# w_o of a one-core hybrid layer: half of its contraction by seven block products

## The chip, the cores and the metric

The kernel runs on one core of a Trainium2 chip. The metric is the device time of one execution in microseconds (us). Before the change the median of 3 runs is 1099.74 us (1099.03 to 1099.78).

## The reference

One layer with D = 1024 on 512 tokens, all in float32:

```
u = rms_norm(h, mix_pre_g);  q, k, v, xr, xg = split(u @ w_in)
y_a = (rg_lru(causal_conv(xr)) * gelu(xg)) @ w_lru_out
y_b = sliding_window_attention(q, k, v, sinks, bias) @ w_attn_out
g = sigmoid(u @ w_gate + b_gate)
merged = g[A] * y_a + g[B] * y_b
h = h + rms_norm(merged @ w_o, mix_post_g)
```

Ahead of this and behind it stands an FFN, h = h + 0.5 * rms_norm((silu(x @ w1) * (x @ w3)) @ w2), with x = rms_norm(h). The change is in `merged @ w_o`, a product of 512 x 1024 by 1024 x 1024.

## The kernel before

**Splitting.** Each float32 operand is held as a high part (rounded to the format that TensorE takes) and a low part (the rest). A product is three matmuls: high by high, high by low, low by high. ACT makes the high part by a copy, DVE the low part by a subtraction. Weights come tile by tile (128 x 1024): SP loads the raw tile (L150), ACT and DVE split it (L191, L192), in the order of a list that `get` walks through. `split2` (L226, L227) does the same for other operands.

**What sets the order.** The program is written out in Python, one instruction stream for each engine, and each engine runs its stream in order. `point()` is called at steps of the PE stream; `later(n, fn, rank)` has `fn` written out n points later. So the numbers in such calls decide where a piece of ACT, DVE or POOL work stands in its stream.

**Ahead of w_o.** Eight groups (tile f, L237 to L239, 24 matmuls of 128x512 each) multiply the attention's output by w_attn_out. Behind each group `mg_out` merges the branches: two DVE steps (L1780, L1781), then the high part on ACT (L1783) and the low part on DVE (L1784), which give tile mg. Each mg is one contraction tile of w_o. In this time the first pair of FFN2 weights (w1b, w3b) is prepared as well: POOL forms sums of raw w1b blocks (L890 to L896), and ACT and DVE split them (`pairs_b.prep`).

**w_o itself** (`tok_gemm`, L255 to L257, tile acc). The output is token major: 4 token tiles of 128 by 2 column halves of 512, so 8 banks of PSUM. All 8 contraction tiles are done classically: 8 x 4 x 2 x 3 = 192 matmuls of 128x512, the last two contraction tiles token by token. When a token tile is done, its norms follow (ACT sums of squares L310 and L334, DVE L311, L322 and so on), then transposes (tr, L355) into uT. The first four groups of FFN2 (tiles 0 and 1 of w1b and w3b) fill PE while the norms run.

**Block products.** For FFN1's w2 and FFN2's w2 a class `Halves` does part of the contraction by seven products in place of eight (Strassen and Winograd). It pairs contraction tiles p and q and views them as a 2 x 2 block matrix: b11, b12, b21, b22 of 2 x 128 rows by 512 columns, and the activations (hEO) as even and odd halves of 256 tokens. Weight blocks are combined as b12 - b11 and so on: `T` copies a block with factor -1 on ACT (L653), and a DMA that adds, issued by POOL, brings the other block from DRAM (L654). Activation sums are DVE steps `S` (L649). A unit (`unit`, L732 to L734, tile hw) is one product: 2 x 2 x 3 = 12 matmuls of 128x512 for one pair. `out` copies banks to SBUF (tile hc), and the norms add them later.

A tile of `BY_CAST` comes without a raw tile: POOL issues a DMA that rounds on the way (L147, high part), ACT writes the negative (L172), and a second POOL DMA adds the original to it (L174, low part).

Of the kernel before, what the change touches and what calls it, by code (L numbers as in the profile page):

```python
# [51 lines left out]
def hybrid_layer(ctx: ExitStack, tc: tile.TileContext, a: dict, out: bass.AP):  # L52
# [80 lines left out]
    want("wo", range(8))  # L133
# [162 lines left out]

    def post_norm(acc, t, gpost, scale, dst, after=None, last=False, eps=D * EPS, mid=None, part=None, ns=(0, 1)):
# [3 lines left out]
        junk = slot([P, D], name="junk")  # L301
# [24 lines left out]
    def norms(acc, t, gpost, scale, gpre, spill, eps, mid=None, part=None, ns=(0, 1)):  # L326

        hg = slot([P, D], name="hg")
        junk = slot([P, D], name="junk")
# [48 lines left out]
    def tok_gemm(nm, xs, n, R, gpost_name, scale, gpre_name, first, x_to=None, xf=None, spill=False, then=None, eps=None, pre=None):  # L378
# [35 lines left out]
        ep = lambda t: D * EPS if eps is None else eps[:, t : t + 1]  # L414
# [19 lines left out]
        if pre:  # L434
            G = pre.G
            pre.hooks[3 * G].append(vectors)
            pre.hooks[4 * G + 2].append(lambda: act.activation(small(1, "tiny"), veps[:, 0:1], AF.Abs_reciprocal_sqrt))
            pre.hooks[4 * G].append(lambda: act.activation(g[1], g[1], AF.Copy, scale=NEWT))
            x0 = st["get"] + len(tail)
            for i, u in enumerate(X_AT):  # L440
                pre.hooks[u].append(lambda i=i: dma_to(x0 + i + 1))
# [7 lines left out]
            for t in range(2):  # L449
                acc[t] = [pre.bank["bc"][t], pre.bank["bx"][t]]  # L450
                for n_ in range(2):
                    classical(t, n_)
            pre.prep(5 * G + LEAD + 2)
            x_split(0)
            norm(0, lambda: x_split(1))
            pre.cap = 7 * G - 2
            for u in range(5 * G, 6 * G):
                pre.step(u)
            pre.cap = 7 * G
            for t in range(2, 4):  # L460
                acc[t] = [pre.bank["bu"][t - 2], bank("acc")]
                classical(t, 1)
            pre.prep(7 * G)
            pre.hid.eo.clear()
            x_split(2)
            norm(1)
            for u in range(6 * G, 7 * G):
                pre.step(u, (0,))
            trs[0] = transpose_mm(us[0])
            transpose_out(trs[0], 0)  # L470
            classical(2, 0)
            for u in range(6 * G, 6 * G + 2):
                pre.step(u, (1,))
# [5 lines left out]
            for u in range(6 * G + 2, 7 * G):  # L479
                pre.step(u, (1,))  # L480
# [1392 lines left out]
GPOST_AT = 26  # L1873


RO = 6

NC1 = 4

# [56 lines left out]
```

## Time and profile before

| | |
|---|---|
| median of 3 runs | 1099.74 us |
| profiled execution | 1099.59 us |
| its span | 1097.7 us |
| granted TensorE clock | 0.998 |
| eight groups of w_attn_out | 670.98 to 714.53 us |
| w_o, classical products | 714.53 to 759.84 us, transposes among them |
| first matmul of FFN2's pairs | 784.14 us |

A row of the timeline gives start, length, engine, line, operation and tiles; a bracket behind it is the time that the engine stood idle before, and what ended that. Matmuls overlap, so the distance of two starts is their price, and not the length in the row. "Landing" is the time from the issue of a DMA to the arrival of its data.

### The profile page before, as it was taken

What the parts mean: (1) busy time and instruction counts of PE and PEld (TensorE: products, weight loads), DVE (VectorE), ACT (ScalarE), POOL (GpSimd) and SP (SyncE); (2) the same over time, 40 slices, a digit from 0 to 9 for tenths busy, and PEclk for the clock granted to TensorE, in tenths of its full rate; (3) what the DMA queues carried; (4) which work ended last, traced back from release to release, by engine and by line L of the source; (5) the groups of instructions that cost most, each with busy time, mean ns of one, the idle gap of its engine ahead of it and who ended that gap; (6) DMA issues with size and microseconds to landing.
All of it is one profiled execution on the core that took longest, in us unless ns stands there. A gap on an engine that the chain in (4) does not pass through costs nothing.

```text
span 1097.7 us, 18111 instructions
## 1 busy us (share of the span) xinstructions
PE 1089.5 (99%) x6856; PEld 986.9 (90%) x6856; DVE 927.0 (84%) x1334; ACT 704.0 (64%) x1226; POOL 398.3 (36%) x352
## 2 busy tenths in 40 slices
PE   9999999999999999999999999999999999999997
PEld 8899999998889878899888888888999999998885
DVE  5887999989997998887778866767889989889996
ACT  7756555588767778656656654446555455578872
POOL 0144933232102513242444443010977656633200
PEclk9999999999999999999999999999999999999999
DMA  9325663389866652157232335452323323449923
GB/s 339 122 81 140 126 158 100 115 184 232 238 167 210 162 151 74 39 178 242 65 91 79 117 133 211 138 187 88 126 78 116 106 88 110 144 103 241 211 77 134
DMA packets 53895, 156.46 MB, mean 143 GB/s; under 512 B 5536, under 2 KB 7456, under 8 KB 53808
## 3 DMA queue, kind: packets, MB, share of 16 engines
q1 hardware_dynamic: 40272, 122.49, 33.0%
q0 software_dynamic: 13248, 32.29, 15.7%
q8 instruction: 54, 0.88, 0.3%
q10 hardware_dynamic: 288, 0.52, 0.1%
q14 instruction: 33, 0.27, 0.1%
HBM read 139.57 MB, written 13.62 MB: 140 GB/s over the span
## 4 chain that ended last, share of the span: by engine, by line
PE 99%; DMA 0%; DVE 0%; ACT 0%; issue 0%; DVEq 0%; ACTq 0%
PE c L842 13%; PE c L843 13%; PE c L844 13%; PE f L237 10%; PE f L238 10%; PE f L239 9%; PE hw L732 6%; PE hw L733 6%; PE hw L734 6%; PE acc L257 1%; PE acc L255 1%; PE acc L256 1%; PE pt L1696 1%; PE s L1660 1%; PE s L1659 1%; PE tr L355 1%
## 5 line engine op out<-in xcount | busy, mean ns | idle before, releaser
L843 PE MATMUL c<-uT,wlo 128*128 128x256 f32 x516 | 146.0, 283 | 0.0
L844 PE MATMUL c<-uT,whi 128*128 128x256 f32 x516 | 146.0, 283 | 0.0
L842 PE MATMUL c<-uT,whi 128*128 128x256 f32 x516 | 146.0, 283 | 0.0
L842 PE MATMUL c<-Xh,whi 128*128 128x256 f32 x504 | 142.7, 283 | 0.0
L843 PE MATMUL c<-Xh,wlo 128*128 128x256 f32 x504 | 142.6, 283 | 0.0
L237 PE MATMUL f<-uT,whi 128*128 128x512 f32 (+1 forms) x380 | 138.5, 364 | 0.0
L238 PE MATMUL f<-uT,wlo 128*128 128x512 f32 (+1 forms) x380 | 136.9, 360 | 0.0
L239 PE MATMUL f<-uT,whi 128*128 128x512 f32 (+1 forms) x380 | 136.9, 360 | 0.0
L844 PE MATMUL c<-Xl,whi 128*128 128x256 f32 x456 | 129.1, 283 | 0.0
L227 DVE TENSOR_TENSOR wlo<-S,whi 128x1024 fp32r<-128x1024 f32 x86 | 120.9, 1406 | 4.7 <-ACT whi L226 2.5
L226 ACT ACTIVATE whi<-S 128x1024 fp32r<-128x1024 f32 x86 | 88.5, 1055 | 29.1 <-DVE S L891 28.0
L843 PEld LDWEIGHTS c<-uT,wlo 128*128 128x128 f32 x516 | 99.0, 192 | 0.2
L842 PEld LDWEIGHTS c<-uT,whi 128*128 128x128 f32 x516 | 99.0, 192 | 0.2
L844 PEld LDWEIGHTS c<-uT,whi 128*128 128x128 f32 x516 | 99.0, 192 | 0.0
L842 PEld LDWEIGHTS c<-Xh,whi 128*128 128x128 f32 x504 | 96.8, 192 | 0.3 <-issue 0.3
L843 PEld LDWEIGHTS c<-Xh,wlo 128*128 128x128 f32 x504 | 96.8, 192 | 0.0
L734 PE MATMUL hw<-whi,uT 128*128 128x512 f32 x228 | 88.7, 389 | 0.0
L732 PE MATMUL hw<-whi,uT 128*128 128x512 f32 x228 | 88.7, 389 | 0.0
L844 PEld LDWEIGHTS c<-Xl,whi 128*128 128x128 f32 x456 | 87.5, 192 | 0.0
L733 PE MATMUL hw<-wlo,uT 128*128 128x512 f32 x216 | 84.0, 389 | 0.0
L237 PEld LDWEIGHTS f<-uT,whi 128*128 128x128 f32 x380 | 71.8, 189 | 11.8 <-issue 1.4
L239 PEld LDWEIGHTS f<-uT,whi 128*128 128x128 f32 x380 | 71.7, 189 | 11.0
(435 smaller groups left out, 3181.8 us busy)
## 6 DMA issues: line engine op xcount, KB each, us to landing
raw_w1b<-in_w1b_dram SPq DMA_DIRECT2D x22, 512.0 KB, 4.2
raw_w3b<-in_w3b_dram SPq DMA_DIRECT2D x22, 512.0 KB, 4.4
raw_w3a<-in_w3a_dram SPq DMA_DIRECT2D x21, 512.0 KB, 4.4
raw_w1a<-in_w1a_dram SPq DMA_DIRECT2D x20, 512.0 KB, 4.5
raw_w2a<-in_w2a_dram SPq DMA_DIRECT2D x17, 512.0 KB, 5.5
raw_wg<-in_wg_dram SPq DMA_DIRECT2D x16, 512.0 KB, 4.1
raw_w2a<-in_w2a_dram POOLq DMA_DIRECT2D x15, 512.0 KB, 10.0
raw_w2b<-in_w2b_dram SPq DMA_DIRECT2D x15, 512.0 KB, 6.9
```

What stands on the lines that cost most here:

```text
L226: act.activation(hi, src, AF.Copy)
L227: dve.tensor_tensor(out=lo, in0=src, in1=f32(hi), op=ALU.subtract)
L237: pe.matmul(ps[:, c0:c1], wh[:, s], h_, start=k == 0 and c0 == 0, stop=False, skip_group_check=True)
L238: pe.matmul(ps[:, c0:c1], wl[:, s], h_, start=False, stop=False, skip_group_check=True)
L239: pe.matmul(ps[:, c0:c1], wh[:, s], l_, start=False, stop=k == KT - 1, skip_group_check=True)
L255: pe.matmul(acc[n], x[:, 0, c], wh[:, s], start=first, stop=False, skip_group_check=skip)
L732: pe.matmul(ps, xs[:, 0, j, c], hi[:, j, :], start=start and j == 0, stop=False, skip_group_check=True)
L733: pe.matmul(ps, xs[:, 0, j, c], lo[:, j, :], start=False, stop=False, skip_group_check=True)
L734: pe.matmul(ps, xs[:, 1, j, c], hi[:, j, :], start=False, stop=i == self.G - 1, skip_group_check=True)
L842: pe.matmul(ps, wh[:, s], xh, start=first, stop=False, skip_group_check=True)
L843: pe.matmul(ps, wl[:, s], xh, start=False, stop=False, skip_group_check=True)
L844: pe.matmul(ps, wh[:, s], xl, start=False, stop=k == 3, skip_group_check=True)
```

## The change

The contraction tiles 0 to 3 of w_o go through `Halves` with one pair of pairs (`GS_W`), tiles 4 to 7 stay classical (`TAIL_W`). In order on PE: units u0 to u4 (m1, m5, m2, m6, m3), classical products of token tiles 0 and 1 into the same banks, u5 (m7), classical token tiles 2 and 3 (second half), u6 (m4), with transposes and the remaining classical products between its parts. With `fold`, m2 and m3 behave differently from before: their banks receive the earlier partial sums by a DVE addition in place (L819 in the new numbering), ahead of the classical products, and so the norms of token tiles 0 and 1 don't add them. The norms of tile 1 are written out right behind those of tile 0, with u5 (m7) inside them; those of tile 2 have the second transposes' copies inside.

`mg_out` halves only mg of tiles 4 to 7 into high and low; tiles 0 to 3 go whole into hEO. The factor 0.5 is dropped and made good by 4 times the epsilon in the norms. The weight operands of w_o's units are formed in three ways: `weight` splits a block in SBUF (u1, u3), `fetch` and `rest` take a plain block from DRAM by a rounding and an adding DMA (u0, u2, u4), `T` and `w7` form the combined blocks. The tiles 0 and 1 of w1b and w3b come by `BY_CAST`. The w1b pair's five steps of preparation stand at other points (`PB_AT`, `PBW_AT`), and the loads of h and the splits of wo4 to wo7 in hooks of the units (`MARKS_W`).

```diff
-    want("wo", range(8))
+    want("wo", TAIL_W)
...
+            if pre.fold:
+                for t in range(2):
+                    acc[t] = [pre.bank["bc"][t], pre.bank["bx"][t]]
+                    for n_ in range(2):
+                        classical(t, n_)
+                pre.prep(7 * G)
+                x_split(0)
+                norm(0, lambda: x_split(1))
+                x_split(2)
+                norm(1, lambda: [pre.step(u) for u in range(5 * G, 6 * G)])
+                for t in range(2, 4):
+                    acc[t] = [pre.bank["bu"][t - 2], bank("acc")]
+                    classical(t, 1)
+                pre.hid.eo.clear()
+                for u in range(6 * G, 7 * G):
+                    pre.step(u, (0,))
+                trs[0] = transpose_mm(us[0])
+                transpose_out(trs[0], 0)
+                x_split(3)
+                classical(2, 0)
+                for u in range(6 * G, 7 * G):
+                    pre.step(u, (1,))
+                trs[1] = transpose_mm(us[1])
+                norm(2, lambda: transpose_out(trs[1], 1))
+                for t in range(2):
+                    transpose_xf(trs[t], t, xf)
+                classical(3, 0)
...
+        def w7(self, i):
+            if self.once("w7", i):
+                dve.tensor_tensor(out=self.raw["b11", i], in0=self.raw["b22", i], in1=self.raw["b11", i], op=ALU.subtract)
+
+        def fetch(self, u):
+            b, i = self.OPERANDS[self.names[u // self.G]][0], u % self.G
+            hi, lo = slot([P, 2, 512], F32R, name="whi"), slot([P, 2, 512], F32R, name="wlo")
+            pool.dma_start(out=hi, in_=self.src(b, i))
+            self.parts[u] = hi, lo
+
+        def rest(self, u):
+            b, i = self.OPERANDS[self.names[u // self.G]][0], u % self.G
+            hi, lo = self.parts[u]
+            act.activation(lo, f32(hi), AF.Copy, scale=-1.0)
+            pool.dma_start(out=lo, in_=self.src(b, i), accum_op=ALU.add)
+
+        def weight(self, u):
+            b, i = self.OPERANDS[self.names[u // self.G]][0], u % self.G
+            hi, lo = slot([P, 2, 512], F32R, name="whi"), slot([P, 2, 512], F32R, name="wlo")
+            split2(hi, lo, self.raw[b, i])
+            self.parts[u] = hi, lo
...
-                if m == "m7":
-                    dve.tensor_tensor(out=o, in0=ps, in1=o, op=ALU.add)
+                if m not in ("m1", "m5", "m6"):
+                    dve.tensor_tensor(out=o if m == "m7" else ps, in0=ps, in1=o, op=ALU.add)
...
-        act.activation(m[:, 0, :], t, AF.Copy, scale=0.5)
-        dve.scalar_tensor_tensor(out=m[:, 1, :], in0=t, scalar=0.5, in1=f32(m[:, 0, :]), op0=ALU.mult, op1=ALU.subtract)
-        mg.append(m)
+        if i in TAIL_W:
+            m = mixed.t[i] = slot([P, 2, SEQ], F32R, name="mg")
+            act.activation(m[:, 0, :], t, AF.Copy)
+            later(1, lambda: dve.tensor_tensor(out=m[:, 1, :], in0=t, in1=f32(m[:, 0, :]), op=ALU.subtract), 0)
...
+    half_w.load(1)
+    half_w.loads.pop()
+    half_w.fetch(0)
+    for n, fn in zip(W_AT, (
+        lambda: half_w.t1(0), lambda: half_w.rest(0), lambda: half_w.fetch(2), lambda: half_w.t2(0), lambda: half_w.rest(2),
+        lambda: half_w.weight(1), lambda: half_w.w7(0), lambda: half_w.t4(0), lambda: half_w.prep(1, False), lambda: half_w.prep(2, False),
+        lambda: half_w.weight(3), lambda: half_w.prep(3, False), lambda: half_w.fetch(4), lambda: half_w.prep(4, False), lambda: half_w.rest(4),
+    )):
+        later(n, fn, 2)
...
-RO = 6
+TAIL_W = (4, 5, 6, 7)
+GS_W = ((0, 2),)
+PB_AT = (1, 3, 5)
+PBW_AT = ((3, 2), (4, 3))
+W_AT = (2, 2, 4, 5, 6, 7, 8, 9, 9, 10, 11, 11, 12, 13, 14)
+MARKS_W = (1, 2, 3, 3), (3, 4, 5, 5)
+XW_AT = (1, 2, 3, 4)
```

The first place is POOL's stream while the groups of w_attn_out run. OL is the low part of the attention's output, S are the sums of w1b blocks. Before:

```order
L1732 TENSOR_TENSOR OL_7020<-o_7269,OH_7019 128x2x128
L895 TENSOR_TENSOR S_1458_7369<-raw_w1b_1451_7342 128x512
L896 TENSOR_TENSOR S_1458_7369<-S_1458_7369,raw_w1b_1450_7340 128x512
L890 TENSOR_TENSOR S_1459_7370<-raw_w1b_1450_7340,S_1458_7369 128x512
L891 TENSOR_TENSOR S_1459_7370<-raw_w1b_1450_7340,raw_w1b_1451_7342 128x512
L294 DMA bc_mix_post_g_7749<-in_mix_post_g_dram 128x1024
```

After (raw_wo are the blocks b12, b22 and t4 of w_o in turn, whi and wlo the parts of u0's, u2's and u4's weights):

```order
L968 TENSOR_TENSOR S_1475_7363<-raw_w1b_1450_7340,raw_w1b_1451_7342 128x512
L691 DMA raw_wo_7380<-in_wo_dram 128x2x512
L724 DMA wlo_7347<-in_wo_dram 128x2x512
L717 DMA whi_7424<-in_wo_dram 128x2x512
L691 DMA raw_wo_7452<-in_wo_dram 128x2x512
L724 DMA wlo_7425<-in_wo_dram 128x2x512
L691 DMA raw_wo_7526<-in_wo_dram 128x2x512
L717 DMA whi_7591<-in_wo_dram 128x2x512
L724 DMA wlo_7592<-in_wo_dram 128x2x512
L294 DMA bc_mix_post_g_7700<-in_mix_post_g_dram 128x1024
```

Eight DMAs on w_o now stand behind the sums of w1b, where POOL had nothing; one more (u0's high part, L717) stands ahead of them.

The second place is DVE's stream ahead of the classical products of w_o. Before:

```order
L1780 SCALAR_TENSOR_TENSOR g_7203<-g_7203,f_7612 128x512
L1781 TENSOR_TENSOR g_7203<-g_7203,g_4751 128x512
L1784 SCALAR_TENSOR_TENSOR mg_7684<-g_7203,mg_7684 128x512
L192 TENSOR_TENSOR wlo_7730<-raw_wo_1506_7610,whi_7729 128x1024
L192 TENSOR_TENSOR wlo_7734<-raw_wo_1522_7662,whi_7733 128x1024
```

After (hx is an activation operand of a unit, hw a bank, hc a bank's copy; raw_wo with one number is a block, with two a classical tile; hw_7742 is the bank of token tile 0, first half, hw_7706 its second half):

```order
L227 TENSOR_TENSOR wlo_7724<-raw_wo_7344,whi_7723 128x1024
L227 TENSOR_TENSOR hx_7725<-hEO_7409,hx_7725 128x512
L227 TENSOR_TENSOR wlo_7731<-S_1475_7363,whi_7730 128x1024
L192 TENSOR_TENSOR wlo_7735<-raw_wo_1538_7670,whi_7734 128x1024
L819 TENSOR_TENSOR hw_7742<-hw_7742,hc_7690 128x512
L227 TENSOR_TENSOR wlo_7759<-raw_wo_7526,whi_7758 128x1024
L227 TENSOR_TENSOR hx_7760<-hEO_7410,hx_7760 128x512
L227 TENSOR_TENSOR w_1570_7765<-raw_w1b_1451_7342,w_1570_7765 128x512
L192 TENSOR_TENSOR wlo_7769<-raw_wo_1539_7672,whi_7768 128x1024
L192 TENSOR_TENSOR wlo_7773<-raw_wo_1540_7674,whi_7772 128x1024
L819 TENSOR_TENSOR hw_7706<-hw_7706,hc_7792 128x512
```

The operands of u5 and u6, a split of w1b's sums and the classical tiles wo5 to wo7 now stand ahead of, or between, the two additions.

The third place is PE's stream where the classical products begin. Before:

```order
L239 MATMUL f_7612<-OL_7020,whi_7531 128x512
L255 MATMUL acc_7666<-whi_7570,mg_7396 128x512
L256 MATMUL acc_7666<-wlo_7571,mg_7396 128x512
L257 MATMUL acc_7666<-whi_7570,mg_7396 128x512
L255 MATMUL acc_7667<-whi_7570,mg_7396 128x512
```

After:

```order
L809 MATMUL hw_7707<-whi_7591,hx_7693 128x512
L255 MATMUL hw_7742<-whi_7696,mg_7568 128x512
L256 MATMUL hw_7742<-wlo_7697,mg_7568 128x512
L257 MATMUL hw_7742<-whi_7696,mg_7568 128x512
L255 MATMUL hw_7742<-whi_7734,mg_7609 128x512
L256 MATMUL hw_7742<-wlo_7735,mg_7609 128x512
```

The classical products stood right behind the last group of w_attn_out; now five units stand between, and the products go into banks that the units and the additions have written. The new line numbers L237 to L257 are the old ones; further down the new ones are larger by 5 to 110 (unit L807 to L809 for L732 to L734, `T` L690 and L691 for L653 and L654).

179 lines of the change are left out of this document (108 added, 71 removed).

## The prediction

> **What bounds the kernel now.** I read the page first, then PE's waits, then the stretch of w_o by windows, then single rows.
>
> ```profile
> span 1097.7 us, 18111 instructions
> ...
> PE 1089.5 (99%) x6856; PEld 986.9 (90%) x6856; DVE 927.0 (84%) x1334; ACT 704.0 (64%) x1226; POOL 398.3 (36%) x352
> ...
> PE 99%; DMA 0%; DVE 0%; ACT 0%; issue 0%; DVEq 0%; ACTq 0%
> ```
>
> The chain that ended last is PE from end to end. PE's own waits say the same: one, at the start.
>
> ```profile
> PE w L1152 <- POOL warm L1149: 1.1, 1, 1.1
> ```
>
> So a matmul less is time less, and any wait of PE that the change brings in is time more. Around w_o the windows (us, then busy us and count of PE, PEld, DVE, ACT, POOL, the granted clock, the DMA share, GB/s) show how much the others have to spare:
>
> ```profile
> 680.00:690.00 10.00, 10.00 (x46) 8.29 (x45) 8.25 (x10) 5.06 (x6) 1.23 (x1) 1.00 0.31 100
> 690.00:700.00 10.00, 10.00 (x45) 8.27 (x45) 7.90 (x11) 4.63 (x6) 0.00 (x0) 1.00 0.07 10
> 700.00:710.00 10.00, 10.00 (x46) 8.26 (x44) 6.82 (x9) 3.17 (x4) 0.00 (x0) 1.00 0.60 229
> 710.00:720.00 10.00, 10.00 (x46) 8.28 (x45) 7.96 (x9) 6.29 (x8) 0.00 (x0) 1.00 0.89 327
> 720.00:730.00 10.00, 10.00 (x46) 8.29 (x45) 4.85 (x5) 2.68 (x3) 2.36 (x3) 1.00 0.61 209
> ```
>
> PE never stops, the clock is full, DVE is busy 79% just before w_o and 49% in it. The change puts new DVE work there.
>
> **Part 1: what PE saves.** PE's rows at the borders (start, length, operation):
>
> ```profile
> 670.98 0.40 PE L237 MATMUL f<-OH,whi 128*128 128x512 f32 x1
> ...
> 714.53 0.39 PE L255 MATMUL acc<-whi,mg 128*128 128x512 f32 x1
> ...
> 759.84 0.28 PE L237 MATMUL f<-uT,whi 128*128 128x256 f32 x1
> ...
> 760.91 0.27 PE L355 MATMUL tr<-ident,hg 128*128 128x128 f32 x1
> ```
>
> Between the first two lie 8 groups of 24 matmuls of 128x512: 43.55 / 192 = 0.2268 us each. Between the last two lie nine of 128x256: 1.07 / 9 = 0.119 us. The lengths in the rows (0.39, 0.28) overlap and are not the price. (The Trainium skill, "Perfetto Trace Analysis", Identifying the Most-Contended Engine, says that matmul busy time is a bad metric since matmuls are pipelined; by 0.39 the saving below would be 12 x 0.39 = 4.7 us, by the step it is 2.7, and the step is what these rows measure.)
>
> Classically w_o is 8 x 4 x 2 x 3 = 192 matmuls of 128x512. Now there are 7 units of 12, which is 84, and 4 contraction tiles of 24, which is 96: 180. **Saved 12 x 0.2268 = 2.72 us.** Against it stand the first four w1b and w3b groups, which fill the gaps:
>
> ```profile
> L237 PE MATMUL f<-uT,whi 128*128 128x256 f32 x40 | 11.5, 287 | 0.0
> ...
> L237 PE MATMUL f<-uT,whi 128*128 128x512 f32 x12 | 4.7, 390 | 0.0
> ```
>
> L237, L238 and L239 are one third each, so 36 of them are 512 wide; after the change all are halves of 256: 72 x 0.119 - 36 x 0.2268 = **0.4 us added**. PE's work falls by 2.3 us. With nothing else, 1099.59 (the profiled execution, 0.15 below the median of 1099.74) - 2.3 = 1097.3.
>
> **Part 2: a new wait ahead of the classical products.** Before, DVE had the eight w_o tiles split by 722.5 (717.86 + 4.63, below), ahead of PE's need. Now PE reaches the first classical matmul after five units of 12: 714.53 + 60 x 0.2268 = 728.13, and the second bank (t0, n1) 12 matmuls later, at 730.85. Ahead of these stand wo5 to wo7 split, and the additions of L819 into the banks; in DVE's row order the addition into the second bank is the last of them. DVE works strictly in order, so I follow DVE back from that addition to what starts its run. That is L712 (b22 - b11); I call its start X.
>
> *From X to the addition* DVE has 40 instructions: 11 of 128x1024 and 29 of 128x512. Their prices, and the price of waiting for ACT in between:
>
> ```profile
> 694.78 0.68 DVE L1780 SCALAR_TENSOR_TENSOR g<-g,f 128x512 f32<-128x512 f32 x1
> 695.49 0.69 DVE L1781 TENSOR_TENSOR g<-g,g 128x512 f32<-128x512 f32 x1
> 696.94 0.69 DVE L1784 SCALAR_TENSOR_TENSOR mg<-g,mg 128x512 fp32r<-128x512 f32 x1 [0.76 <-ACT mg L1783]
> ...
> 717.86 4.63 DVE L192 TENSOR_TENSOR wlo<-raw_wo,whi 128x1024 fp32r<-128x1024 f32 x4 [0.26 <-ACT whi L191]
> L744 DVE TENSOR_TENSOR hc<-hw,hc x4: 677/683/690, 319.9 to 1075.7; 128x512 f32<-128x512 f32 x4
> 716.78 3.89 ACT L191 ACTIVATE whi<-raw_wo 128x1024 fp32r<-128x1024 f32 x4
> ```
>
> Four wide splits run in 4.63, so 1.14 apart (the last one is 1.22 long); ACT's four in 3.89, so 0.95 apart. Narrow DVE rows start 0.60 to 0.71 apart; L744, an addition from a bank, is the nearest to L819. So 11 x 1.14 + 29 x 0.64 = 31.1 us busy. Then the waits: where DVE makes a block that ACT must round before DVE can subtract, DVE stands 0.76 (the bracket). By the new rows that happens at eight places: three plain ones (hx of the second sum, two mg) 2.3; one with a wide ACT copy between (0.76 + 0.95) 1.7; one with a narrow one 1.3; around the bank copies of u0 and u1 0.9, 0.3 and 0.8. Together 7.3. So the second addition ends at **X + 38.4**, and PE's wait is X + 38.4 - 730.85 = **X - 692.4**, if that is positive. (wo6 and wo7, split ahead of the second addition, show part of it inside the first bank; it is the same wait.)
>
> *What sets X.* L712 is queued behind the wao5 and whi_u1 splits on DVE, and these on ACT behind the copy (-whi) of u2's weight, which waits for a cast DMA from POOL. POOL issues it after its four sums, a T accumulate and u0's accumulate:
>
> ```profile
> 679.48 1.75 POOL L891 TENSOR_TENSOR S<-raw_w1b,raw_w1b 128x512 f32<-128x512 f32 x1
> ...
> L147 POOL DMA_DIRECT2D whi<-in_xr_dram x4: 531/534/548, 292.8 to 299.1; - x4
> ...
> DMA to landing us min/median/max: 4.3/6.4/7.5
> ...
> L174 POOL DMA_DIRECT2D wlo<-in_xr_dram x4: 851/865/883, 310.0 to 337.0; - x4
> ...
> DMA to landing us min/median/max: 5.7/6.0/6.3
> ...
> L654 POOL DMA_DIRECT2D raw_w2a<-in_w2a_dram x15: 1193/1194/1276, 224.6 to 276.9; - x15
> L654 POOL DMA_DIRECT2D raw_w2b<-in_w2b_dram x2: 1259/1406/1552, 957.3 to 958.3; - x2
> ...
> DMA to landing us min/median/max: 6.4/7.9/9.5
> ...
> DMA to landing us min/median/max: 6.0/10.7/15.8
> ```
>
> Each landing row (least, median, most) belongs to the issues above it, the last one to all 33 of L654. The sums end at 681.2 (681.8 with the 0.53 issue of u0's cast ahead of them). Then 1.19 + 0.87 of issues: the cast starts at 683.9. Alone it lands after 6.4 (690.3); behind two accumulates it is later: the w2b pair, issued 1.2 us apart, landed after 6.4 and 9.5, 4.3 us apart. I take 1.9 for each DMA ahead, below that pair, since here a cast reads no old contents: T at 687.9, u0's at 689.8, the cast at 691.7. From there ACT does -whi (0.95), wao5 (0.95), whi of u1 (1.04), and DVE wao5's low half, two narrow steps and wlo of u1 beside and behind it: 5.9 in all by the steps above, so **X = 697.6**. The other input of L712, T b22, is later than that only if its own landing stretches: ACT copies at 688, POOL issues at 689.0, landing 695.0 to 697. The floor of X is PE's own: whi of u1 needs the room of the fourth gate product's low weights, free after four groups at 670.98 + 4 x 5.44 = 692.7, then 1.04 and 1.14: 694.9. The ceiling by the last row's median, 10.7 a landing, with T b12 and T b22 one behind the other: 681.8 + 10.7 + 1.05 + 10.7 = 704.
>
> (The Trainium skill, "DMA: Bandwidth & Descriptors", Bandwidth, has 1 MB from GpSimd in 6.15 us of transfer; estimated from that, 512 KB take about 3 us, and 4 with the first byte, which would put X on its floor. The rows here, 6.0 and 6.4 for 512 KB, don't agree, and I go by them.)
>
> So the wait is 697.6 - 692.4 = **5.2 us**, between 2.5 (floor) and 11.6 (ceiling). Behind L712 stands all of DVE's later work, behind the waiting L255 all of PE's. The moved transfers don't come last:
>
> ```profile
> h<-h_scr SPq DMA_DIRECT2D x9, 512.0 KB, 4.5
> ...
> raw_wo<-in_wo_dram SPq DMA_DIRECT2D x8, 512.0 KB, 3.8
> ```
>
> wo5 to wo7 are issued on SP behind the last gate product's matmuls, at 711 to 713 by the old clock, so they lie there by 717 to 718; DVE comes to wo5 at X + 30 = 727. The h tiles are issued from u3 on, at 722 or later, and are wanted by the first norm after 736. The steps of w1b's pairs that move into the units (one of the wide splits, one narrow) are among the 40 instructions.
>
> **Part 3: behind it.** The norms of tokens 0 and 1 move with PE and keep the room that they had: ACT and DVE have nothing left over from the splits by then. Between the last classical block and the fourth transposes there was no room before:
>
> ```profile
> 765.33 0.72 ACT L346 ACTIVATE hg<-hg,r 128x512 f32<-128x512 f32 x1 [0.59 <-DVE r L277]
> ...
> 766.81 0.27 PE L355 MATMUL tr<-ident,hg 128*128 128x128 f32 x1
> ```
>
> ACT ends at 766.05, PE comes at 766.81: 0.76 to spare. Now the stored half is added to the bank first (0.68 and a hand-over), and more ACT transposes stand in line: from no wait to 1.3, I take 0.4. The w1b and w3b tiles 0 and 1 come by cast and accumulate on POOL (6.4 + 1 + 6.0, issued some 30 us ahead): nothing. The products of w_o hide it; without that cover PE would wait for what is left of a landing. The gate's scale (4 x eps in place of 0.5) and the shared junk room: nothing.
>
> **Sum:** 1099.59 - 2.3 + 5.2 + 0.4 = **1102.9**, from 1101.8 (X = 696.5, no late wait) to 1105.7 (X = 699.5, 1.3 late).
>
> **The rivals.**
>
> *A. The landings are short and X is on its floor.* A wait of 2.5 to 3 remains and eats the saving: 1099.8 to 1101.1. For it: DMA share is 0.07 in 690:700, so the transfers have the engines to themselves. Against: even the lone rows are 6.0.
>
> *B. No wait at all*, the side opposite to my forecast: faster, 1097.3. It decides at X = 692.4, or at a DVE run of 35.9 in place of 38.4 with X on its floor: then a third of the ACT waits would have to vanish, for instance if ACT rounds further ahead than DVE needs. Against: ACT can't round a block that DVE hasn't formed, and the bracket of 0.76 recurs in every group of before.
>
> *C. The accumulates are slow as in the w2 stages* (median 10.7). X = 702 to 704, wait 9.6 to 11.6: 1106.9 to 1109.5. For it: three accumulates and casts within 3 us. Against: in the w2a stage the DMA share was 1.10 (the row below), here it is 0.31 to 0.07.
>
> ```profile
> 240.00:248.00 8.00, 8.00 (x37) 6.61 (x36) 8.00 (x11) 8.00 (x11) 3.58 (x3) 1.00 1.10 262
> ```
>
> (The Trainium skill, "SBUF — State Buffer", the part on a bandwidth-pool intuition, has a GpSimd DMA go from 620 to 3100 ns beside a DVE copy, since descriptors can't be written; by that X would be up to 5 us later, this rival's time. The issues of L654 keep 1193 to 1276 beside a busy DVE, which speaks against it.)
>
> **How the numbers follow.** Forecast 0.50, A 0.26, B 0.09, C 0.15. A measurement tells apart about 0.2%, 2.2 us: faster means below 1097.5, slower above 1101.9. B is faster but for a tail: 0.08. Slower are C and nearly all of the forecast: 0.15 + 0.46 = 0.61. The rest, A and the lower edge of the forecast, is 0.31. The range takes A's lower end with a little late gain (1099.4) up to the middle of C (1108.0); B and the upper half of C, 0.16, stay out.
>
> **What would show it.** PE's waits should list L255 and L256 on hw, for wo6, wo7 and the L819 additions, some 5 us in a handful of rows, where before there was none, and DVE without a pause over 2 us from L712 to L819. DVE's L712 should start near 697.6 on the old clock of the span, behind a cast landing near 691.7. The w_o stretch should hold 180 matmuls at 0.227. I am wrong if PE shows no wait there (B), if the waits are at the units u1 to u4 themselves (an operand is late, not DVE), or if the time comes from the pairs stage after 784.

## The result and the profile after

| | before | after |
|---|---|---|
| median | 1099.37 us (5 runs, 1099.03 to 1099.78) | 1105.19 us (5 runs, 1102.72 to 1106.74) |
| profiled execution | 1099.59 us, span 1097.7 | 1106.19 us, span 1104.4 |

The ratio is 1.0052 (95% interval 1.0037 to 1.0067): slower by half a per cent. The profiled execution of after lies 1.0 us above its median; its mean granted clock is 0.995, that of the other four runs 0.996 to 0.998, and the run with 0.998 is the fastest. What is read below from this one profile is that much on the dear side.

The head of the page after, and the chain that ended last:

```profile
span 1104.4 us, 18226 instructions
...
PE 1090.3 (99%) x6880; PEld 987.0 (89%) x6880; DVE 929.7 (84%) x1346; ACT 715.4 (65%) x1243; POOL 409.8 (37%) x368
...
PE 91%; DVE 4%; ACT 2%; issue 2%; DMA 1%; POOL 0%; DVEq 0%; ACTq 0%; POOLq 0%
```

PE carried 99% of the chain before and 91% now. PE's waits (us in total, times, longest) say where it was left; before there was one row, the start's:

```profile
PE hw L255 <- DVE hw L819: 2.0, 1, 2.0
PE c L920 <- DVE wlo L227: 1.9, 2, 1.4
PE hw L256 <- DVE wlo L192: 1.1, 1, 1.1
PE w L1229 <- POOL warm L1226: 1.1, 1, 1.1
PE f L1279 <- ACT uT L1272: 0.7, 1, 0.7
PE hw L255 <- ACT whi L191: 0.3, 1, 0.3
```

Three rows on hw stand ahead of the classical products, as foreseen, but sum to 3.4 us. The row on c (a product of the pairs) is in the pairs stage, and was not foreseen. Now the windows of after (us, then busy us and count of PE, PEld, DVE, ACT, POOL, the granted clock, DMA share, GB/s):

```profile
727.00:731.00 4.00, 2.04 (x9) 1.38 (x8) 4.00 (x6) 3.97 (x6) 1.06 (x2) 1.00 0.92 308
731.00:738.00 7.00, 5.60 (x13) 3.57 (x12) 6.03 (x9) 5.54 (x9) 0.88 (x1) 0.52 0.43 134
738.00:745.00 7.00, 7.00 (x32) 5.74 (x31) 3.78 (x11) 3.62 (x9) 0.87 (x1) 0.99 0.54 83
810.00:820.00 10.00, 8.64 (x72) 8.44 (x71) 10.00 (x8) 4.51 (x7) 9.76 (x6) 1.00 0.10 41
```

From 731 to 738 PE did 13 matmuls at a granted clock of 0.52; before, the same window holds 33 at 1.00. The rows of PE there (start, length, operation, in brackets the idle time before it):

```profile
714.26 0.39 PE L807 MATMUL hw<-whi,hx 128*128 128x512 f32 x1
...
727.64 0.39 PE L809 MATMUL hw<-whi,hx 128*128 128x512 f32 x1
729.98 0.50 PE L255 MATMUL hw<-whi,mg 128*128 128x512 f32 x1 [1.96 <-DVE hw L819]
...
732.11 0.80 PE L255 MATMUL hw<-whi,mg 128*128 128x512 f32 x1 [0.26 <-ACT whi L191]
734.04 0.79 PE L256 MATMUL hw<-wlo,mg 128*128 128x512 f32 x1 [1.14 <-DVE wlo L192]
...
735.91 0.63 PE L257 MATMUL hw<-whi,mg 128*128 128x512 f32 x1
736.34 0.63 PE L255 MATMUL hw<-whi,mg 128*128 128x512 f32 x1
...
745.37 0.39 PE L807 MATMUL hw<-whi,hx 128*128 128x512 f32 x1
```

The units end at 727.87. 48 classical matmuls by 0.2268 are 10.9 us, so u5 (745.37) was due at 738.75: **6.6 us lost**. The reader sees two kinds of loss. First, DVE's lateness (its rows stand below): the addition into bank (t0, n1), which is token tile 0, second column half, is the first of the two in DVE's last row and ends at 735.7, where PE was due at 730.59, 5.1 late. Second, matmuls 0.43 apart (735.91 to 736.34) in place of 0.23: PE comes to that bank only at 736.34, 0.6 after it is ready, and loses 0.9 more until 738.3. So **5.1 is DVE, 1.5 the slow clock**.

In after's chain of work (start, length, what), the cast of u2's weight, which releases DVE's run:

```profile
681.59 9.85 DMA whi<-in_wo_dram
```

DVE's rows from X to the second addition:

```profile
697.24 1.22 DVE L712 TENSOR_TENSOR raw_wo<-raw_wo,raw_wo 128x1024 f32<-128x1024 f32 x1
...
732.77 2.35 DVE L192 TENSOR_TENSOR wlo<-raw_wo,whi 128x1024 fp32r<-128x1024 f32 x2
735.04 1.29 DVE L819 TENSOR_TENSOR hw<-hw,hc 128x512 f32<-128x512 f32 x2
```

The second piece of time is in the pairs stage. Its first matmul and the fourth transposes ahead of it (they read hg, the last token tile when its norm is done), before:

```profile
766.81 1.04 PE L355 MATMUL tr<-ident,hg 128*128 128x128 f32 x8
...
784.14 0.28 PE L842 MATMUL c<-uT,whi 128*128 128x256 f32 x1
```

and after:

```profile
774.79 1.06 PE L360 MATMUL tr<-ident,hg 128*128 128x128 f32 x8 [0.22 <-DVE hg L350]
...
788.65 0.28 PE L919 MATMUL c<-uT,whi 128*128 128x256 f32 x1
```

Before, 17.33 us lay between the two, now 13.86. In this time DVE and POOL make the first operands of the pairs. The windows between these rows, before and then after, show that PE never stops in either (their counts take in the eight transposes and matmuls that reach over the ends):

```profile
766.81:784.14 17.33, 17.33 (x116) 15.90 (x114) 12.52 (x10) 9.41 (x14) 13.40 (x6) 1.00 0.51 167
...
774.79:788.65 13.86, 13.86 (x117) 13.86 (x117) 10.09 (x9) 9.24 (x14) 9.91 (x5) 1.00 0.47 152
```

So the distance is set by PE's order. `tok_gemm` writes the first four groups of w1b and w3b in another order when it is given `pre`, as it now is for w_o (that code is older, and so not in the diff). By PE's rows 51 narrow matmuls (128x256) of these groups stood ahead of the fourth transposes before and 84 stand there now; behind them stood 69 narrow and 36 wide ones, and now 108 narrow. The 33 that went ahead are 33 x 0.119 = 3.9 us; 72 narrow in place of 36 wide give 0.4 back: 3.5. They could not simply go behind again, since hg came 0.22 us after PE even so.

The stage itself, from its first matmul to the end of the span, took 1097.7 - 784.14 = 313.6 us before and 1104.4 - 788.65 = 315.8 after: **2.2 us lost**.

The books of the two profiled executions: 1099.59, less 0.27 (w_o begins at 714.26, not 714.53), less 2.3 of PE's work, plus 5.1, plus 1.5, plus 0.5 between u5 and the pairs (0.2 of it the bracket at 774.79), plus 2.2, is 1106.3. It took 1106.19.

### The profile page after: what moved, and what is told of

It reads as the page before. It is cut to its first block, busy times and chain, and to the rows that moved or that the text cites. A ratio compares the mean times of both kernels' runs of the same rounds, so it can differ in the third digit from the quotient of the medians.

```text
span 1104.4 us, 18226 instructions
## 1 busy us (share of the span) xinstructions
PE 1090.3 (99%) x6880; PEld 987.0 (89%) x6880; DVE 929.7 (84%) x1346; ACT 715.4 (65%) x1243; POOL 409.8 (37%) x368
## 4 chain that ended last, share of the span: by engine, by line
PE 91%; DVE 4%; ACT 2%; issue 2%; DMA 1%; POOL 0%; DVEq 0%; ACTq 0%; POOLq 0%
PE c L920 13%; PE c L919 13%; PE c L921 13%; PE f L237 8%; PE f L238 8%; PE f L239 8%; PE hw L807 6%; PE hw L808 6%; PE hw L809 6%; PE pt L1774 1%; DMA whi<-in_wo_dram 1%; DVE wlo L227 1%; PE hw L256 1%; PE s L1738 1%; PE hw L257 1%
## 5 line engine op out<-in xcount | busy, mean ns | idle before, releaser
L237 PE MATMUL f<-uT,whi 128*128 128x512 f32 (+1 forms) x392 | 140.6, 359 | 0.0
L239 PE MATMUL f<-uT,whi 128*128 128x512 f32 (+1 forms) x392 | 139.0, 355 | 0.0
L807 PE MATMUL hw<-whi,uT 128*128 128x512 f32 x228 | 88.7, 389 | 0.0
L809 PE MATMUL hw<-whi,uT 128*128 128x512 f32 x228 | 88.7, 389 | 0.0
L237 PEld LDWEIGHTS f<-uT,whi 128*128 128x128 f32 x392 | 74.1, 189 | 11.4 <-issue 1.4
L239 PEld LDWEIGHTS f<-uT,whi 128*128 128x128 f32 x392 | 74.1, 189 | 10.5
```

What stands on the lines that cost most here:

```text
L237: pe.matmul(ps[:, c0:c1], wh[:, s], h_, start=k == 0 and c0 == 0, stop=False, skip_group_check=True)
L239: pe.matmul(ps[:, c0:c1], wh[:, s], l_, start=False, stop=k == KT - 1, skip_group_check=True)
L807: pe.matmul(ps, xs[:, 0, j, c], hi[:, j, :], start=start and j == 0, stop=False, skip_group_check=True)
L809: pe.matmul(ps, xs[:, 1, j, c], hi[:, j, :], start=False, stop=i == self.G - 1, skip_group_check=True)
```

## The experiments

Two theories, each with a rival. **D**: the wait ahead of the products is the length of DVE's run from b22 - b11 (X) on; rivals: the slow clock is a loss of its own, or the bank additions are what counts. **E**: the pairs stage loses time because the fourth transposes come too close ahead of it; rival: an order within the stage. In every trace I read the same three stretches, each from start to start within the one profiled execution: from the first matmul of the units to the first of u5 (108 matmuls, 24.5 us at full speed), on to the first of the pairs, and on to the end of the span. The runs of after and of the kernels with 4 executions overlap in time, so for pool1, warm, nofold, norms_late, pbw5 and xf_after it is the stretches that tell, more than the medians. The profiled executions of pbw5 and best2 were the dearest of their kernels (1106.35 and 1100.10); what they have above the median lies ahead of the units, which begin at 716.66 and 716.08 in them and near 714.2 in the others.

| run | units to u5 | u5 to pairs | pairs to end | median |
|---|---|---|---|---|
| after | 31.1 | 43.3 | 315.8 | 1105.19 |
| late_u56 | 26.9 | 43.3 | 316.0 | 1101.81 |
| pool1 | 31.0 | 43.3 | 315.7 | 1105.15 |
| warm | 30.3 | 43.3 | 315.6 | 1105.26 |
| both | 25.3 | 43.3 | 315.6 | 1100.27 |
| pad | 25.6 | 45.4 | 313.2 | 1100.12 |
| xf_mid | 25.5 | 43.1 | 313.8 | 1098.65 |
| nofold | 31.4 | 43.3 | 316.1 | 1106.17 |
| norms_late | 30.0 | 43.3 | 315.7 | 1105.76 |
| pbw5 | 28.2 | 43.9 | 315.7 | 1103.74 |
| xf_after | 30.3 | 43.1 | 314.0 | 1103.87 |
| best | 24.5 | 44.3 | 314.0 | 1099.09 |
| best2 | 24.5 | 43.5 | 314.2 | 1098.55 |

**late_u56.** u5's and u6's operands, which stood inside DVE's run, are formed behind the bank additions.

```diff
-    half_w = Halves("wo", mixed, hooks_w, GS_W, 0, True, 4)
+    half_w = Halves("wo", mixed, hooks_w, GS_W, 0, True, 1)
...
+    hooks_w[1].insert(0, lambda: half_w.prep(5))
```

> The operands of u5 and u6 (two wide and two narrow DVE steps) are formed behind the additions into the banks instead of ahead of them; u4 is prepared where it was. Theory D (DVE's run from L712 to the second bank addition sets PE's wait): the run shrinks by 2 x 1.14 + 2 x 0.61 = 3.5 us, the second addition ends near X + 34.9 = 732.1, PE loses about 1.5 us at the first classical products in place of 6.6, and its clock stays at 1.00; time 1100.1 to 1101.7. Rival P (PE waits for something else there, a landing of a w_o tile or a bank): 1104 to 1106 as with the change.

Measured 1101.81, ratio 1.0024 (1.0015 to 1.0034), 0.1 above the range expected. The first stretch is 4.2 shorter, the other two are as they were. PE's first wait is now

```profile
PE hw L255 <- DVE hw L819: 0.7, 1, 0.7
```

and the window of 730 to 740 has a granted clock of 1.00 where after has 0.66. D holds: DVE work taken out of the run comes off PE's wait, and the slow clock goes with it.

**pool1.** POOL issues the three DMAs on which X seemed to hang ahead of w1b's sums.

```diff
-PB_AT = (1, 3, 5)
+PB_AT = (3, 4, 6)
-W_AT = (2, 2, 4, 5, 6, 7, 8, 9, 9, 10, 11, 11, 12, 13, 14)
+W_AT = (1, 2, 1, 5, 6, 7, 8, 9, 9, 10, 11, 11, 12, 13, 14)
```

> POOL issues T b12, the cast of u2's weight and u0's accumulate ahead of the four sums of w1b instead of behind them; the sums and the splits of them come one to two points later. Theory D: the cast lands some 4 to 5 us sooner, X (L712) goes from 697.2 to PE's floor near 694.9, the wait shrinks by 2.3 us; time 1101.5 to 1103. Rival: X hangs on another input (T b22, or a room that DVE or PE gives free later): L712 moves by less than 0.5 us and the time stays at 1104 to 1106.

Measured 1105.15, no gain: the rival, in its range and with its sign. DVE's and POOL's rows of this run show why:

```profile
687.00 2.28 POOL L968 TENSOR_TENSOR S<-raw_w1b,raw_w1b 128x512 f32<-128x512 f32 x1
689.22 1.20 POOL L691 DMA_DIRECT2D raw_wo<-in_wo_dram  x1
...
696.76 1.23 DVE L712 TENSOR_TENSOR raw_wo<-raw_wo,raw_wo 128x1024 f32<-128x1024 f32 x1 [0.35 <-DMA raw_wo<-in_wo_dram]
```

The sums, now later, run beside DVE's splits and take up to 2.28 us each in place of 1.3. The next DMA (b22) stands behind them, is issued at 689.22 and lands at 696.7. X moves by 0.5 us only (0.3 against the start of the units): the other input of L712, which the prediction put just behind the cast, takes the place of the cast.

**warm.** 23 idle matmuls among the first products keep PE busy (their results go nowhere).

```diff
+                        for k, d in zip(tail, ((9, 0, 10, 2), (2, 0, 0, 0))[n_]):
+                            warm(d)
+                            mm_tok(accs(t), xs[k], t, w[k], False, k == tail[-1], (n_,), True)
```

> 23 matmuls of 128x512 whose result nobody reads are put into PE's gaps ahead of and inside the first two banks' classical products (9, 10, 2 and 2); nothing else changes. Theory C (a pause of PE lowers the granted clock afterwards, and that costs time of its own): the clock stays at 1.00 between 730 and 740, the matmuls there keep 0.227 us, the classical products end about 1.5 us sooner than with the change, time 1103.0 to 1104.2 with a small spread. Rival: the slow clock is hidden behind DVE's additions and norms anyway: time 1104.5 to 1106.

Measured 1105.26, within 0.1 of after, and so the rival by its range. The trace says more: the granted clock stays 1.00, PE has no wait at the products, and the first stretch is 30.3, which is 24.5 and 0.6 and the 5.2 that 23 matmuls cost. So 5.8 is enough to cover DVE's lateness (5.2 in this profile), against 6.6 in the profile of after: at least 0.8 there is the clock. On the median nothing is gained, since the idle matmuls cost 5.2 in every run (1105.16 to 1105.39), while after's runs differ by 4 us.

**both** (late_u56 and pool1 together).

> late_u56 and pool1 together. Theory D: the second addition ends near 694.9 + 34.9 = 729.8, ahead of PE at 730.6: no wait ahead of the classical products, clock 1.00. Left are 2.3 us less PE work, 0.4 us small waits, and the 1.9 us that PE lost in the pairs stage near 815: 1099.0 to 1100.0. If the loss in the pairs stage came from the late w_o stage and goes with it: 1097.3 to 1098. Rival P: 1103 to 1106.

Measured 1100.27, ratio 1.0013 (1.0004 to 1.0022). The first stretch is down to 25.3, 0.8 above its least. The third is still 315.6: the loss of the pairs stage doesn't depend on the wait at the products. At 2.1 us it is more than the 0.9 by which this kernel is behind the one before.

**pad** (on both): nine idle matmuls between the last w1b and w3b group and the first pairs product.

```diff
+            if pre.fold:
+                fill = bank("dm")
+                for _ in range(9):
+                    pe.matmul(fill, ws[3][0][:, 0:P], uT[:, 0, 0, :], start=True, stop=True, skip_group_check=True)
```

> This is the kernel of run both (1100.27) with nine idle products of 128x512, 2.04 us of TensorE time, put between the last w1b and w3b group and the first pairs product; their results go nowhere. Theory E: in the pairs stage VectorE and GpSimd are the bound from 778 to 822, and PE, which begins 1.5 us sooner relative to the transposes than they can follow, catches up with them at 815 and waits 1.9 us there. Then the 2.0 us of idle products only take the place of that wait: PE's rows 'c <- DVE wlo' fall from 1.9 to under 0.3, and the time stays at 1100.0 to 1100.9. Rival: the stage hangs on PE, each step triggered by PE's evictions, and the 1.9 us wait comes from a fixed order in it; then the wait stays and the time is 1102.0 to 1102.6.

Measured 1100.12. 2.1 us of matmuls were added ahead of the stage, the stage became 2.4 shorter, PE's rows on c are gone, and the time is that of both. E holds, the rival (1102.0 to 1102.6) falls: PE came too early, and DVE and POOL, not an order among PE's steps, set when it can go on.

**xf_mid** (on both): the copies of the first two transposed tiles go into norm 2, and nine narrow matmuls go behind the fourth transposes.

```diff
-                norm(2, lambda: transpose_out(trs[1], 1))
-                for t in range(2):
-                    transpose_xf(trs[t], t, xf)
+                norm(2, lambda: [transpose_out(trs[1], 1), transpose_xf(trs[0], 0, xf), transpose_xf(trs[1], 1, xf, (0,))])
+                transpose_xf(trs[1], 1, xf, (1,))
...
+            k0 = range(1 if pre.fold else KT // 2)
             start(k0)
+            k1 = range(len(k0), KT)
```

> This is the kernel of run both (1100.27) with the ACT copies of the first two transposed tiles moved ahead into norm 2 (where ACT idles 1.5 us waiting for DVE's h), so that norm 3's first square no longer waits 1.2 us behind them, and with nine narrow products (1.07 us) moved from ahead of the fourth transposes to behind them. Nothing is left out. Theory E (pairs stage bound by VectorE and GpSimd, which start when the fourth transposes are out): the distance from these transposes to the first pairs product grows from 13.9 to 14.9 us, the wait at the pairs shrinks from 1.9 to about 0.9, and the time is 1099.0 to 1099.7. Rival: the wait hangs on the order within the pairs and stays 1.9, time 1100.0 to 1100.6. Third outcome: norm 3 isn't sooner, PE waits about 1 us for hg at the fourth transposes: 1100.3 to 1101.3.

Measured 1098.65, better than expected: ratio 0.9996 (0.9987 to 1.0005). The waits on c fall from 1.9 to

```profile
PE c L922 <- DVE wlo L227: 0.2, 1, 0.2
```

In both, ACT's rows showed four copies ahead of norm 3's first square, whose input DVE had had ready at 760.7:

```profile
760.00 2.04 ACT L380 ACTIVATE xf<-tr 128x512 f32<-128x512 f32 x4
761.91 0.65 ACT L315 ACTIVATE junk<-hc 128x512 f32<-128x512 f32 x1
```

**xf_after**: the same edit on the changed kernel itself.

> The changed kernel (1105.2) with only the edit of run xf_mid: the ACT copies of the first two transposed tiles ahead in norm 2, nine narrow products from ahead of the fourth transposes to behind them. Theory: the loss in the pairs stage (1.9 us of PE's waits for wlo, 2.2 us from the first pairs product to the end) is a term of its own that has nothing to do with the wait ahead of the classical products; it falls to 0.2 to 0.4 and the time is 1103.3 to 1103.9. Rival: since the waits and the slow clock of the products have already moved the norms, ACT's copies aren't on the way of norm 3 here, and PE waits for hg at the fourth transposes: 1105.0 to 1106.0.

Measured 1103.87, 1.3 below after, and the third stretch falls by 1.7 to 314.0, while the wait ahead of the products is still there. The pairs loss is a term of its own.

**nofold**: the partial sums of tokens 0 and 1 are added in the norms, not into the banks.

```diff
-            if t < 2 and self.fold:
-                return None
...
-            if u % self.G == self.G - 1 and m in ("m1", "m5", "m6", "m7") + (("m2", "m3") if self.fold else ()):
+            if u % self.G == self.G - 1 and m in ("m1", "m5", "m6", "m7"):
```

> The changed kernel (1105.2) with the partial sums of tokens 0 and 1 not added into the banks ahead of the classical products, but added inside the norms, as in the older layout; all else stays. Theory D (the wait is DVE's run from b22 - b11 to the second addition): four additions of 0.64 leave the run ahead of wo7's split, two of them ahead of the first product; PE's row 'hw L255 <- DVE hw' is gone, the wait for wo6 and wo7 splits stays at about 3.6 to 4.0 in place of 5.1, the slow clock behind it is shorter. Norms 0 and 1 become 1.4 us longer each and have 8 us to spare ahead of the transposes. Time 1103.2 to 1104.4. Rival: the banks' additions are what PE waits for, and without them the products run: loss under 1.5 us, time 1099.8 to 1101. Other rival: it moves nothing, since norms pay back what the products gain: 1104.8 to 1105.6.

Measured 1106.17: none of the three ranges. PE's waits change their names, and hardly their sum (3.8, in after 3.4):

```profile
PE hw L255 <- ACT whi L191: 2.0, 1, 2.0
PE hw L256 <- DVE wlo L192: 1.8, 2, 1.0
```

The two additions ahead of the first product are 1.2 us less for DVE, which then waits for ACT:

```profile
730.46 1.23 DVE L227 TENSOR_TENSOR wlo<-raw_wo,whi 128x1024 fp32r<-128x1024 f32 x1 [0.78 <-ACT whi L226]
...
732.80 2.35 DVE L192 TENSOR_TENSOR wlo<-raw_wo,whi 128x1024 fp32r<-128x1024 f32 x2
```

wo7's split ends at 735.15, in after at 735.12. Of the 1.2, 0.8 became the wait for ACT, and 0.4 is that DVE's run was already later in this execution, as the same step in after and then in nofold shows:

```profile
725.22 1.23 DVE L227 TENSOR_TENSOR wlo<-raw_wo,whi 128x1024 fp32r<-128x1024 f32 x1 [0.69 <-ACT whi L226]
...
725.58 1.23 DVE L227 TENSOR_TENSOR wlo<-raw_wo,whi 128x1024 fp32r<-128x1024 f32 x1 [0.69 <-ACT whi L226]
```

ACT has no pause from there on either (rounding, bank copies, and a table load of 1.28 at 727.62 in after). So theory D needs a correction: the run is one of DVE *and* ACT, and work that burdens DVE alone can leave it with little gain, here 0.4 of 1.2. late_u56 took out work of both engines. In the time nothing was gained.

**pbw5**: one wide and one narrow split of w1b's pair, which burden both engines, go from u2 and u3 to u5.

```diff
-PBW_AT = ((3, 2), (4, 3))
+PBW_AT = ((3, 5), (4, 5))
```

> The changed kernel (1105.2) with one wide and one narrow split of the first w1b pair (VectorE 1.14 and 0.60 a step, ACT the rounding of each) moved from the units u2 and u3 to u5, behind the classical products. Theory D (TensorE's wait ahead of the classical products is the length of VectorE's run from b22 - b11 on): wo7's split ends 1.74 us sooner, the loss from the last unit to u5 falls from 6.6 to between 3.4 (slow clock gone) and 4.9, time 1102.0 to 1103.5. Rival: ACT, without a pause in 723 to 734, is the bound as VectorE's runs are shortened, as the run without bank additions hints, and gives back what VectorE gains: 1104.3 to 1105.2.

Measured 1103.74, 0.2 above the range of D and below its rival's. The first stretch is 2.9 shorter: 1.6 of DVE's run, whose addition into the second bank is 3.5 late in place of 5.1, and 1.3 of the clock, which stays at 1.00 from 727 to 745. The splits now lie within norm 1, and 0.6 comes back as a wait at the fourth transposes (0.8, after 0.2).

**norms_late**: norm 1 goes back behind u5 and the products (2,1) and (3,1) (token tile, column half), which undoes the change's last words.

```diff
-                x_split(2)
-                norm(1, lambda: [pre.step(u) for u in range(5 * G, 6 * G)])
+                for u in range(5 * G, 6 * G):
+                    pre.step(u)
                 for t in range(2, 4):
                     acc[t] = [pre.bank["bu"][t - 2], bank("acc")]
                     classical(t, 1)
+                x_split(2)
+                norm(1)
```

> The changed kernel (1105.2) with the norm of token tile 1 put where it stood in the older order, behind u5 and the products (2,1) and (3,1), in place of ahead of them; all else stays. It undoes the change's last words alone. My theory: norm 1 starts when its bank is complete, at about 743, and its transposes come at 760; TensorE doesn't wait for it, but norm 2 and norm 3 follow it on VectorE and ScalarE in a row of 8.5 us each, so if norm 1 begins 3 us later PE waits for the later norms: 1106.5 to 1109. Rival: the norms have room in the products, the order doesn't matter: 1104.8 to 1105.7.

Measured 1105.76, 0.06 above its rival's range and 0.6 above after, inside the spread of both (4 and 5 runs): the place of norm 1 makes no difference that can be told. I had expected 1106.5 or more. The second stretch is the same 43.3.

The first stretch of this run says something that it was not made for. From 690 up to the second bank addition DVE and ACT have the same rows, in the same order, as in after, and DVE is as late (5.3, after 5.1); but the stretch is 30.0 in place of 31.1. What differs is the clock: it fell here too, but came back sooner. PE's row behind the pause, and two windows:

```profile
730.10 0.73 PE L255 MATMUL hw<-whi,mg 128*128 128x512 f32 x1 [2.12 <-DVE hw L821]
...
731.00:733.00 2.00, 2.00 (x6) 1.32 (x4) 2.00 (x4) 2.00 (x3) 0.00 (x0) 0.50 1.05 375
736.00:738.00 2.00, 2.00 (x10) 1.68 (x10) 1.20 (x3) 0.69 (x2) 0.88 (x1) 1.00 0.34 25
```

In after the clock is still 0.50 from 736 to 738. So the slow clock costs 0.2 us in this profile and 1.5 in that of after, with the same work ahead of it.

**best** (late_u56, pool1, xf_mid and pbw5 in one kernel).

> All that the runs have shown to pay, in one kernel: u5's and u6's operands behind the bank additions, the GpSimd order of run pool1, the copies of run xf_mid (1098.65) and the w1b splits of run pbw5. What is left of TensorE's waits in xf_mid are 0.4 us listed and some 0.5 in gaps of 0.1 to 0.2 at the classical products, where wo6 and wo7 come just in time; VectorE's run gets 1.74 us shorter, so these go. Expected 1097.6 to 1098.2, a ratio of 0.9984 to 0.9990 to the kernel before. Rival: the moved splits now fall into the norms ahead of the fourth transposes or into the pairs stage and cost there what they gain: 1098.4 to 1099.2.

Measured 1099.09, the rival. The first stretch is at its least, 24.5; the second pays 1.2 back:

```profile
767.93 1.09 PE L360 MATMUL tr<-ident,hg 128*128 128x128 f32 x8 [1.19 <-DVE hg L350]
```

**best2**: as xf_mid, with the wide split alone between norm 0 and norm 1, and ACT's copy for a w1b cast in its place inside norm 1.

```diff
                 norm(0, lambda: x_split(1))
-                x_split(2)
-                norm(1, lambda: [pre.step(u) for u in range(5 * G, 6 * G)])
+                pre.early()
+                norm(1, lambda: [x_split(2)] + [pre.step(u) for u in range(5 * G, 6 * G)])
...
+    half_w.early = lambda: pairs_b.prep(0, 3)
...
-PBW_AT = ((3, 2), (4, 3))
+PBW_AT = ((4, 3),)
```

> The kernel of run xf_mid (1098.65) with one wide w1b split moved from u2 to the place between norm 0 and norm 1, where VectorE stands 1.5 us in the run best (bracket 1.52), and ACT's copy for the third w1b cast behind norm 1's root, where ACT stands 2.85 us; the narrow split stays in the units. VectorE's run ahead of wo7 gets 1.14 us shorter. If the products' remaining gaps of about 1 us in xf_mid hang on that run and the norms don't pay it back, u5 starts at 738.7 to 739.0 on a span where the units start at 714.2, PE waits less than 0.3 for hg at the fourth transposes, and the time is 1097.7 to 1098.3. Rival: the chain of three norms in a row pays back every bit that the products gain, as in run best; PE waits 0.6 to 1.2 for hg: 1098.5 to 1099.2.

Measured 1098.55, 0.25 above the range and inside the rival's, with a wait of 0.4 at the transposes, between the signs of the two: ratio 0.9990 (0.9981 to 0.9999). It is the one version that is faster than the kernel before with an interval that excludes 1, by 0.8 us of 1099.3. It excludes it narrowly, and twelve kernels were measured, so the gain is likely but not firm. Its advantage over xf_mid (0.1) is not shown.

## Why the prediction was right, and where it was not

1. **PE's work, -2.3.** Right. Where nothing is late (best, best2) 108 matmuls take 24.5 us, the 0.2268 each that the working used.
2. **X = 697.6.** Measured 697.24, with the cast at 691.44 (foreseen 691.7). The landing time was right by two errors that cancel: POOL's sums ended at 680.1 and not at 681.8, and the issues behind them stood closer, so the cast was issued at 681.59 and not at 683.9; and it took 9.85 us behind the two adding DMAs, not 7.8.
3. **The run of 38.4 us.** Measured 38.4 (697.24 to 735.7, half of the last row). The wait from it is 5.1, foreseen 5.2. That wo6 and wo7 would show part of it was right. The eight waits for ACT in it were right as well: 7.0 us by the brackets of DVE's rows, foreseen 7.3. What the working missed is that ACT is as full from 720 on: in nofold, where DVE has less to do, it waits 0.8 us for ACT.
4. **The wait's price.** Taken as the idle time alone. The granted clock fell to half from 732 to 738, which cost 1.5 us more in the profile; warm bounds it from below at 0.8, and norms_late has the same work with 0.2. This term was missing.
5. **Behind it, 0.4.** Measured 0.5. But the working looked no further than the wait at the transposes. It priced the first w1b and w3b groups by their number and not by their place: 33 narrow matmuls more stand ahead of the fourth transposes, which brought these 3.5 us closer to the pairs, and there 2.2 us were lost. The prediction named the pairs stage as what would make it wrong, and put no price on it. pad, xf_mid and xf_after show the term: more room ahead of the stage takes it away. xf_mid, which takes ACT's copies out of norm 3's way, could put nine of the matmuls back behind the transposes without a wait there.

So the forecast had its main wait right, in place and in size, partly by luck in point 2, and left out two terms. 1102.9 is 2.3 us short of the median; the two missing terms are 3.7 in the profiled execution, which itself lies 1.0 above that median. Of the rivals, A (X on its floor) and B (no wait) fall by the 5.1 us; C (slow accumulates, X = 702 or more) falls by X.

How DVE and POOL hold each other up is seen in the pairs stage of after, in DVE's rows: a split beside POOL's sums, and one while POOL stands idle (its sums begin again at 827.86):

```profile
796.10 2.31 DVE L227 TENSOR_TENSOR wlo<-S,whi 128x1024 fp32r<-128x1024 f32 x1
...
826.56 1.22 DVE L227 TENSOR_TENSOR wlo<-raw_w1b,whi 128x1024 fp32r<-128x1024 f32 x1 [2.13 <-ACT whi L226]
```

and in POOL's, where the backlog ends:

```profile
820.14 2.27 POOL L968 TENSOR_TENSOR S<-raw_w3b,raw_w3b 128x512 f32<-128x512 f32 x1
827.86 2.29 POOL L972 TENSOR_TENSOR S<-raw_w1b 128x512 f32<-128x512 f32 x1 [5.45 <-DVE wlo L227]
```

A sum of POOL's while DVE stood idle (674.95 to 680.47) took 1.31:

```profile
678.82 1.31 POOL L968 TENSOR_TENSOR S<-raw_w1b,raw_w1b 128x512 f32<-128x512 f32 x1
```

2.31 against 1.22, and 2.27 against 1.31: each nearly doubles the time of many of the other's steps as long as both have work, until 822. (The Trainium skill, "SBUF — State Buffer", Who interferes with whom, says that a VectorE instruction with two SBUF inputs contends with a GpSimd instruction that reads SBUF. The rows agree.) So 3.5 us less of a head start isn't made up, and PE catches up at 819. Before, POOL's first pause in this stage came earlier:

```profile
800.78 2.30 POOL L895 TENSOR_TENSOR S<-raw_w1b 128x512 f32<-128x512 f32 x1 [2.51 <-DVE wlo L227]
```

From 770 on POOL had worked off a backlog there without a pause, and was through at 798, with no wait of PE's. That row was there to be read ahead of the change: behind 3.5 us less of a head start POOL's backlog lasted from 778 to 822. How much of the head start PE could have spared, no run measures.

What stays open: the clock's share on the median, since the runs of after differ by 4 us and only one execution of each kernel has a trace (its size differs between executions, as norms_late shows); why the cast took 9.85 us; and the 1.5 us between best2 and the 1097.1 that the saved matmuls would give. Of these, 0.7 stands in the third stretch and 0.7 in the first two (68.0 us, where the kernel before needs 69.6 for the same way, less 2.3); what each is made of was not followed up.

## What to carry to other kernels

When PE is the bound and an edit moves work to DVE, follow both DVE and ACT to the last operand that PE needs: where they hand work to each other, relieving one gains little. Then follow the edit past its own stage, to the next place where an engine works off a backlog, since a lead that shrinks there is paid for 40 us later. For that, count not only the filler matmuls on PE but where in its order they stand. A wait of PE can cost more than its idle time: here one of 2 us lowered the clock, and what that cost differed from execution to execution.

## What the hardware showed that I had not expected

PE's clock fell after short pauses. In after it stood 2.0 us and did six matmuls, the last of them already slow (the row of 731.25 is 0.60 long, those ahead of it 0.40); it stood 0.3 and 1.1 more, and the window of 732 to 738 has

```profile
732.00:738.00 6.00, 4.75 (x10) 3.38 (x11) 5.03 (x8) 4.54 (x8) 0.88 (x1) 0.50 0.33 99
```

in the granted clock's column 0.50. In norms_late the matmuls right behind one pause of 2.1 were slow (0.43 apart, where 0.23 is the full clock's), and from 734 the clock was full again. With pauses of 0.9, 1.2 and 0.2 (pbw5) it stayed at 1.00; with 1.2, 0.5 and 1.4 (xf_after) it was 0.76 from 732 to 739. (The Trainium skill, "TensorE: Matmul & The Clock Gate", What's actually happening, puts the fall to half speed after an idle window of some 3.4 us. Here the longest pause was 2.1, so by the skill's rule no clock would have been lost; the trace decides.) The other surprise is GpSimd's cast of 512 KB, which took 9.85 us behind two adding DMAs on its queue, and 4.2 at the least.
